# Output projection of a decoder layer: seven half-size products with sums of its weights kept in DRAM

## The chip, the cores and the metric

The kernel runs on one NeuronCore of a Trainium2 chip. A core has five engines with queues of their own: TensorE (PE, matmul), VectorE (DVE), ScalarE (ACT), GpSimd (POOL) and SyncE (SP, which issues nearly all DMAs here), and 16 DMA engines. The metric is the device time of one execution in microseconds; smaller is better. Several runs are taken and their median is compared.

## The reference

One layer of a decoder trunk, 1024 tokens, width 1024, all float32:

```
x = x + 1/2 * SwiGLU_1(RMSNorm(x))
z = RMSNorm(x) @ W_in                        # u, v, c_q, c_kv, k_rope, q_mem, three gates
y_a, y_b, y_c = spatial gating, latent attention, memory attention
merged = sum_i sigmoid(gate_i) * (y_i @ W_branch_i)
x = x + merged @ W_out                       # 1024 x 1024 by 1024 x 1024
x = x + 1/2 * SwiGLU_2(RMSNorm(x))
```

## The kernel before, in words

**Matmul in three parts.** Values are float32, but PE is fed fp32r operands. Each operand is split into `hi` (a cast on ACT) and `lo` (source minus `hi`, on DVE); `split`, L138 to 142. A product is three matmuls, hi hi, hi lo and lo hi, added up in PSUM (`mm3`, L155 to 161). One matmul here has 128 rows of stationary weights and 512 moving columns (tokens).

**Layout.** Activations are feature by token: 8 tiles of 128 features, in two halves of 512 tokens. `Rows` holds the residual stream as `[half, p]`, a tile of 128 x 2 x 512 for two feature tiles.

**Stages in order.** FFN 1 up (`up`, units of two feature columns), FFN 1 down (`down`, 7 loops of 6 steps), the gate and latent projections (`Gates`), mixer branches A and C with attention B among them, branch B with the merge, the output projection (`project`, L1143), FFN 2 up and down. Up, down and gates already are seven half-size products instead of eight (`Seven`, L1398): a 2 x 2 block product is made from seven products of sums of blocks, where the sums of weights (`sums`, names s1 to s4) and of rows (t1 to t4) are made on DVE.

**Branch B and projection before.** `branch_pairs` (L553) makes for each of 8 feature tiles and 2 token halves the product of attention's output with `w_branch` (4 k-steps of 3 matmuls), multiplies it with the gate rows on DVE (L573), adds what branches A and C left (`mc`) on POOL (L574) and splits the result into `merged`. `project` then runs over 2 token halves and 8 output tiles: it loads and splits a column of `w_out` (128 x 1024, again for each half), makes 8 k-steps of 3 matmuls into one PSUM bank, adds the bank to the residual rows (L1155), and calls `norm.feed` (a square on ACT, an addition into the norm's accumulator on DVE, L1302 and L1307). In the second half it runs the norm of the first half as tasks: `sums` (token sums by four PE transposes and a reduce, then an inverse root of ten small DVE operations), `turn` (four PE transposes that spread the scale over partitions, L425), and `part(0)`, `part(1)`: gain and scale on four row pairs (L1344), a difference (L1367) and splits (L147), which give the operands `b22` and `t3` for the first unit of FFN 2.

**The first units of FFN 2** (`units`, L1522) begin with the products of `t3` and `b22`. After `count + 1` = 3 of their k-steps PE takes the token sums of half 1 (`norm.tokens(1)`, L394), so that norm's chain runs beside the rest of these products.

**What sets the order.** Tile's scheduler places instructions by priority (program order) and a model of time; inside `manual_schedule` the engines named keep the written order. In `down` of FFN 1 that is PE, SP, DVE and ACT; in `project` and branch B none. In `down` each step writes: the matmuls of the step, the operand differences (L2101, L2105), the splits for the next step (`prepare`), the row additions due (`acts`), and then what a table `post` holds for that (loop, step); `pre` comes ahead of the matmuls. `pre` at (5, 2) has the norm's token sums (PE transposes at L410). `post` at (1, 0) and (1, 4) fetches gate unit 0 and makes its four sums (L1443). Each step also does a little of the rotary tables.

**Room.** Tags have fixed numbers of buffers: `raw` 3, `whi` and `wlo` 5 each, `t` (rows of 512) 6, `h4` 16, `x4` 10, `w4` 11 (in each FFN's own pool), PSUM `bank` 4 and `one` 4.

**Small jobs.** `rounded` (L691) loads a tile of weights, splits it and stores both parts to DRAM, in two steps at two units; `weight_jobs` (L716) lays them over the units of the first up projection, `Gates.run` others over its units. `spill` (L2061) makes differences of hidden rows on POOL after every second unit.

## Time and profile before

| | |
|---|---|
| median of 3 runs | 2162.38 us (2162.04 to 2163.84) |
| profiled execution | 2163.03 us, of which the span from first to last instruction is 2161.3 |
| granted PE clock | 0.999 |
| up 1, down 1, gates | about 116 to 440, 440 to 651, 651 to 960 us |
| branch B, projection | 1395 to 1440, 1440 to 1527 us |
| DVE busy in 1398 to 1441, to 1484, to 1527 | 38.4, 21.7, 32.7 us of 43 each |

The profile is one execution, seen by the hardware. Its page gives busy time by engine, the chain of work that ended last, and the costliest groups of instructions. Rows of the timeline read: start, time, engine, line, operation, output<-inputs, shape, count, and in brackets how long the engine had been idle and what released it. Busy durations of matmuls overlap, since a matmul starts before the one ahead has left the array; the distance of starts is what one costs.

### The profile page before, as it was taken

The page shows a single profiled execution, that of the slowest core. Times are in us where ns is not written, and L with a number is a line of the kernel's source. Part 1 is how long each engine was busy: PE and PEld are TensorE (multiplying, and loading weights), DVE is VectorE, ACT ScalarE, POOL GpSimd, SP SyncE. Part 2 cuts the span into 40 slices and gives each one's busy share as a digit, 9 for nine tenths or more (in the row PEclk, how much of TensorE's full clock was granted, in tenths as well). Part 3 has the DMA queues.
Part 4 walks back from the last instruction along what each step waited for, and adds up shares of the span by engine and source line. Part 5 has one row for each costly group of instructions (what it writes and reads, how often), then busy time and mean ns, then how long its engine had stood idle before and what let it go on. Part 6 is the DMA issues. An engine that isn't in the chain of part 4 may idle for free.

```text
span 2161.3 us, 27448 instructions
## 1 busy us (share of the span) xinstructions
PE 2151.9 (100%) x10112; PEld 1797.8 (83%) x10112; DVE 1572.1 (73%) x2371; ACT 910.3 (42%) x1486; POOL 255.0 (12%) x256
## 2 busy tenths in 40 slices
PE   9999999999999999999999999999999999999999
PEld 6888888888887888888988889988888888888887
DVE  7966666679889657655786679886876666657884
ACT  6433333243455434433555378833433223224332
POOL 0011111100000000000123311240011212110000
PEclk9999999999999999999999999999999999999999
DMA  4264555385332445641587832293133332347443
GB/s 148 92 220 159 190 180 175 119 318 193 118 124 94 147 164 180 223 149 61 212 283 259 314 105 69 75 348 104 40 127 103 110 97 100 103 144 288 169 129 104
DMA packets 137175, 342.56 MB, mean 158 GB/s; under 512 B 21713, under 2 KB 30033, under 8 KB 137041
## 3 DMA queue, kind: packets, MB, share of 16 engines
q1 hardware_dynamic: 136896, 340.81, 45.9%
q8 instruction: 79, 1.29, 0.2%
q14 instruction: 56, 0.45, 0.1%
q10 hardware_dynamic: 144, 0.00, 0.0%
HBM read 230.90 MB, written 109.86 MB: 158 GB/s over the span
## 4 chain that ended last, share of the span: by engine, by line
PE 91%; DVE 6%; ACT 1%; DMA 1%; issue 1%; SPq 0%; POOL 0%; ACTq 0%; DVEq 0%; POOLq 0%
PE one L158 15%; PE one L159 15%; PE one L160 15%; PE bank L158 13%; PE bank L159 13%; PE bank L160 13%; PE mm L158 1%; PE mm L159 1%; PE mm L160 1%; PE bank L1019 1%; PE one L1967 1%; DVE w L147 1%; DVE wlo L147 1%; DVE pr L997 1%; DVE wlo L142 1%
## 5 line engine op out<-in xcount | busy, mean ns | idle before, releaser
L146 ACT CAST whi<-x 128x1024 fp32r<-128x1024 f32 x202 | 192.3, 955 | 414.4 <-DVE x L1443 170.4
L147 DVE TENSOR_TENSOR wlo<-x,whi 128x1024 fp32r<-128x1024 f32 x202 | 241.2, 1195 | 58.9 <-ACT whi L146 19.6
L1471 DVE TENSOR_TENSOR t<-t,one 128x512 f32<-128x512 f32 x188 | 128.9, 686 | 190.8 <-PE one L160 190.7
L158 PE MATMUL bank<-h,whi 128*128 128x512 f32 x636 | 247.9, 390 | 0.0
L160 PE MATMUL bank<-h,wlo 128*128 128x512 f32 x636 | 247.5, 389 | 0.0
L159 PE MATMUL bank<-h,whi 128*128 128x512 f32 x636 | 247.5, 389 | 0.0
L158 PE MATMUL one<-h,whi 128*128 128x512 f32 x508 | 199.0, 392 | 0.0
L159 PE MATMUL one<-h,whi 128*128 128x512 f32 x508 | 198.4, 390 | 0.0
L160 PE MATMUL one<-h,wlo 128*128 128x512 f32 x508 | 198.3, 390 | 0.0
L158 PE MATMUL one<-w,whi 128*128 128x512 f32 x432 | 168.5, 390 | 0.0
L159 PE MATMUL one<-w,whi 128*128 128x512 f32 x432 | 168.1, 389 | 0.0
L160 PE MATMUL one<-w,wlo 128*128 128x512 f32 x432 | 168.1, 389 | 0.0
L142 DVE TENSOR_TENSOR wlo<-w,whi 128x1024 fp32r<-128x1024 f32 (+2 forms) x112 | 114.4, 1036 | 67.3 <-ACT whi L139 67.1
L139 ACT CAST whi<-w 128x1024 fp32r<-128x1024 f32 (+2 forms) x112 | 98.8, 901 | 149.8 <-PE one L159 55.6
L2067 POOL TENSOR_TENSOR raw<-raw 128x512 f32<-128x512 f32 x38 | 57.0, 1499 | 794.8 <-DVE raw L1908 684.8
L160 PEld LDWEIGHTS bank<-h,wlo 128*128 128x128 f32 x636 | 119.4, 188 | 24.9
L159 PEld LDWEIGHTS bank<-h,whi 128*128 128x128 f32 x636 | 119.4, 188 | 24.6
L158 PEld LDWEIGHTS bank<-h,whi 128*128 128x128 f32 x636 | 119.4, 188 | 24.4
L158 PE MATMUL bank<-whi 128*128 128x512 f32 x352 | 136.9, 389 | 0.0
L159 PE MATMUL bank<-wlo,whi 128*128 128x512 f32 x352 | 136.9, 389 | 0.0
L160 PE MATMUL bank<-whi,wlo 128*128 128x512 f32 x352 | 136.9, 389 | 0.0
L160 PEld LDWEIGHTS one<-h,wlo 128*128 128x128 f32 x508 | 95.8, 189 | 20.1
(406 smaller groups left out, 4892.2 us busy)
## 6 DMA issues: line engine op xcount, KB each, us to landing
x<-in_ffn_w_gu_dram SPq DMA_DIRECT2D x78, 512.0 KB, 5.1
w<-tdt SPq DMA_DIRECT2D x40, 512.0 KB, 4.2
gate<-raw SPq DMA_DIRECT2D x33, 512.0 KB, 3.0
tdb<-raw SPq DMA_DIRECT2D x64, 256.0 KB, 2.1
h<-in_ffn_w_down_dram SPq DMA_DIRECT2D x64, 256.0 KB, 6.0
w<-tdb SPq DMA_DIRECT2D x30, 512.0 KB, 5.1
tdt<-w SPq DMA_DIRECT2D x48, 256.0 KB, 2.4
x<-in_w_gate_dram SPq DMA_DIRECT2D x22, 512.0 KB, 5.9
```

The source lines that it names most:

```text
L139: i = self.nc.scalar.copy(hi, src)
L142: return (eng or self.nc.vector).tensor_tensor(lo, src, hi.bitcast(F32), op=ALU.subtract)
L146: self.nc.scalar.copy(hi, src)
L147: return lambda: self.nc.vector.tensor_tensor(lo, src, hi.bitcast(F32), op=ALU.subtract)
L158: i = mmul(out, s[0], m[0], start=first, stop=False, **kw)
L159: mmul(out, s[0], m[1], start=False, stop=False, **kw)
L160: self.last = mmul(out, s[1], m[0], start=False, stop=last, **kw)
L997: nc.vector.tensor_tensor_reduce(out=pr[:, :m], in0=sc[:, :m], in1=self.mask[:, m0:m0 + m], scale=1.0, scalar=-NEG, op0=ALU.add, op1=ALU.m ...
L1019: nc.tensor.transpose(b[:, at:at + P], prs[t][:, kk * P:(kk + 1) * P], self.ident)
L1471: return self.nc.vector.tensor_tensor(out, x, y, op=ALU.add)
L1967: k.last = nc.tensor.matmul(b, w, norm.x(half, c), start=c == 0, stop=c == DT - 1)
L2067: sub = lambda d, x, y: (eng or nc.gpsimd).tensor_tensor(d, x, y, op=ALU.subtract)
```

## The change

The projection becomes seven products too: `merge` replaces the last call of `branch_pairs` and `project`. With A the blocks of W_out and b those of `merged` (b11 is features 0 to 511 of token half 0, b12 of half 1, b21 and b22 the other features), it makes b11 A11, t2 s2, t1 s1, b22 s4, t3 s3, b21 A12 and t4 A22, each into four banks of 512 tokens with 4 k-steps. A bank that is used by more than one output is added with its sign into several rows. The residual halves change names (norm half 0 is now token half 1), and `store` follows.

The sums s1 to s4 of W_out's blocks are made from DRAM to DRAM, by DMAs on POOL's queue that copy or add (`out_sums`: eight steps of two 512 KB transfers, one step at every odd unit of the first up projection). All seven weight blocks are then split and stored as hi and lo in DRAM by 14 jobs: three in the up projection, eight in `down` (`out_jobs`, split at every second step from (2, 3) to (4, 5)), three in the gates. `merge` only loads them.

Moved: the fetch and the four sums of gate unit 0 go from (1, 0) and (1, 4) to (4, 4) and (5, 1) of `down`; x1d's rows, and the fetch of FFN 2's first weights, from ahead of the projection to places in `merge`; FFN 2's first sums and "t" splits from `units` into `merge` (`later`). The branch additions go from POOL to DVE. PE is in written order in `merge`. The turned sums and the scale of norm half 0 use PSUM tag `one`.

The core of the diff (`weights(n)` in it loads the hi and lo of block n, `add` adds a bank to a row, `put` splits rows into an operand):

```diff
+        sums = self.out_sums()
+        self.wo_parts = self.out_parts()
+        wo = [self.rounded(x.unsqueeze(1), d) for x, d in self.wo_parts[:2] + self.wo_parts[10:11]]
-        for first, some in ((0, jobs), (1, small)):
+        for first, step, some in ((0, 2, jobs), (1, 2, small), (13, 2, wo[:2]), (16, 1, wo[2:])):
...
+        for n, f in enumerate(sums):
+            when[2 * n + 1].append(f)
...
+    def out_sums(self):
+        self.wosum = [self.dram.tile([2, P, D], F32, name=f"wosum{n}") for n in range(4)]
+        A11, A12, A22, A21 = range(4)
+        w, (s3, s1, s2, s4) = self.a["w_out"], self.wosum
+        steps = ((s3, A11, None), (s1, A21, None), (s3, A21, 1), (s1, A22, 1),
+                 (s2, s3, None), (s2, A22, 1), (s4, s2, None), (s4, A12, 1))
+        def step(d, src, more):
+            for g in range(2):
+                x = w[g, src] if isinstance(src, int) else src[g]
+                self.nc.gpsimd.dma_start(d[g], x, max_dma_last_dim=2 * D, **({"accum_op": ALU.add} if more else {}))
...
+    def out_jobs(self, parts):
+        def job(src, dst):
+            x = self.raw()
+            self.nc.sync.dma_start(x, src)
+            yield
+            hi, lo = self.wide("whi"), x.bitcast(F32R)
+            self.split(hi, lo, x)
+            for d, t in zip(dst, (hi, lo)):
+                self.nc.sync.dma_start(d, t.bitcast(F32))
+            yield
+        when = {}
+        for i, part in enumerate(parts):
+            j, q = job(*part), 11 + 2 * i
+            for at, k in ((q, 1), (q + 4, 0)):
+                when.setdefault(at, []).append((k, lambda j=j: next(j)))
...
+    def merge(self, yb, mc, room, norm, load, early, later, sink):
...
+        raw = {n: [room() for _ in range(2)] for n in names}
...
+        def branch(name, k):
...
+            sig, d = self.row(), raw[name][k // 2]
+            nc.sync.dma_start(sig, self.sig[DT + dt][:, hf])
+            if k % 2 == 0:
+                nc.sync.dma_start(d, mc[dt:dt + 2, :, hf].rearrange("k p t -> p k t"))
+            b = self.bank()
+            self.branch(b, w[dt], yb, hf)
+            tt(sig, sig, b, op=ALU.mult)
+            tt(d[:, k % 2], d[:, k % 2], sig, op=ALU.add)
...
+        load()
+        w2 = weights(1)
+        for u, b in product("a", self.single, ws, "b11", True):
+            add(1, 2 * u + 1, b, ALU.subtract)
...
+        for u, b in product("y", self.bank, ws, "t3", True):
+            add(0, 2 * u + 1, b)
+            norm.feed(0, 2 * u + 1)
+            sink(0, 2 * u + 1)
+        ws = weights(6)
+        later()
+        norm.take = self.single
+        for u, b in product("a", None, w2, "b21", False):
+            add(1, 2 * u, b)
+            if u == 1:
+                with self.tc.high_priority(offset=600):
+                    norm.sums(0)
+            elif u == 3:
+                norm.turn(0)
+                norm.take = None
+                norm.part(0)
+            norm.feed(1, 2 * u)
+        for u, b in product("y", None, ws, "t4", False):
+            parts = 2 if u == 3 else 1
+            if u == 0:
+                norm.part(1)
+            add(1, 2 * u + 1, b, parts=parts)
+            norm.feed(1, 2 * u + 1, parts)
+            sink(1, 2 * u + 1)
...
-                    {(1, 0): [do(gates.first, 0)], (1, 4): [do(gates.sums, 0)],
+                    {(4, 4): [do(gates.first, 0)], (5, 1): [do(gates.sums, 0)],
...
-                    late)
+                    late, self.out_jobs([*self.wo_parts[2:10]]))
...
+            def later():
+                for f in range(2):
+                    ffn.sums(f)
+                    made[f] = ffn.weights(f, "t")
+            with tc.manual_schedule(engines={mybir.EngineType.PE}):
+                self.merge(yb, mc, ffn.w4, norm, load, early, later, lambda half, c: keep(x2d, norm.t, half, c))
...
-                    (0, 1), (), ([(0, "a")], [(1, "a")]),
+                    (0, 1), made, ([(0, "a")], [(1, "a")]),
...
+        wo = [k.rounded(x.unsqueeze(1), d) for x, d in k.wo_parts[11:]]
+        jobs = {0: [rows], 1: [rows], 2: [wo[0]], 3: [wo[0], wo[1]], 4: [wo[1], mem[0]], 5: [mem[0], pairs[0]],
+                6: [pairs[0]], 7: [mem[1]], 8: [mem[1], pairs[1]], 9: [pairs[1]], 10: [cq], 11: [cq],
+                12: [wo[2]], 13: [wo[2]]}
```

More of the change, by code (lines that the diff above doesn't have):

```diff
@@ L399, in token_sums, with turned_sums @@
         return b
-    def turned_sums(self, acc, parts=1, late=False):
+    def turned_sums(self, acc, parts=1, late=False, bank=None):
         nc, n = self.nc, acc.shape[-1] // P
@@ L407, in turned_sums @@
             m = min(4, n - t0)
-            b = self.bank()
+            b = (bank or self.bank)()
             for t in range(m):
@@ L1136, in mixer @@
         yb = self.attention(self.branch_pairs(2, yc, md, self.x4, first + each[8:], sink_c))
[L1137 to L1162 removed]
+        return yb, mc
@@ new lines, in out_sums @@
+    def out_sums(self):
[8 more added lines that the diff above has]
+                self.nc.gpsimd.dma_start(d[g], x, max_dma_last_dim=2 * D, **({"accum_op": ALU.add} if more else {}))
+        return [lambda x=x: step(*x) for x in steps]
@@ L1291, in __init__ @@
         self.acc, self.r, self.s, self.op, self.rows = {}, {}, {}, {}, {}
-        self.more = []
+        self.more, self.take = [], None
     def feed(self, half, c, parts=1):
@@ L1320, in tokens @@
         if half == 0 and not self.scaled:
-            self.s[half] = k.turned_sums(self.acc.pop(half), late=True)
+            self.s[half] = k.turned_sums(self.acc.pop(half), late=True, bank=self.take)
         else:
@@ L1333, in turn @@
         k = self.k
-        self.s[half] = k.norm_scale(self.r[half], late=k.last is not None)
+        self.s[half] = k.norm_scale(self.r[half], late=k.last is not None, bank=self.take)
     def norm(self, half, p):
@@ L1712, in run @@
                     self.row_weights(range(5), [w4, x4, x4, x4, x4])
-                self.extra += self.later[:1] + [lambda x=x: got.append(next(x)) for x in jobs.get(n, ())]
+                self.extra += self.later[:1] + [lambda x=x: got.extend(y for y in [next(x)] if y is not None) for x in jobs.get(n, ())]
                 del self.later[:1]
@@ L2085, in up, with down @@
                     self.spill(f // 2)
-    def down(self, rows, load, sink, pre={}, post={}, aside=iter(())):
+    def down(self, rows, load, sink, pre={}, post={}, aside=iter(()), jobs={}):
         k, nc, KT = self.k, self.nc, self.KT
@@ L2184, in loop @@
                     prepare(n + 1, 0)
-                for act in [*acts[n, s], *post.get((n, s), ())]:
+                for act in [*acts[n, s], *post.get((n, s), ()), *jobs.get((n, s), ())]:
                     act()
```

139 lines of the change are left out of this document (103 added, 36 removed).

## The prediction

> **What bounds the kernel now.** I read the page's busy line and chain first, then TensorE's waits, then windows over the stages that the change touches, then the timeline of VectorE (DVE) in them.
>
> ```profile
> PE 2151.9 (100%) x10112; PEld 1797.8 (83%) x10112; DVE 1572.1 (73%) x2371; ACT 910.3 (42%) x1486; POOL 255.0 (12%) x256
> PE 91%; DVE 6%; ACT 1%; DMA 1%; issue 1%; SPq 0%; POOL 0%; ACTq 0%; DVEq 0%; POOLq 0%
> ```
> ```profile
> PE bank L231 <- POOL ident masks.py:199: 1.5, 1, 1.5
> PE one L158 <- DVE raw L1471: 0.7, 2, 0.5
> ```
>
> TensorE (PE) is the whole chain, and its longest wait after the start is 0.5 us. So a matmul less is worth its full spacing, and anything late at PE costs its full lateness. No slack elsewhere pays for either.
>
> ```profile
> 1516.20 0.39 PE L159 MATMUL bank<-h,whi 128*128 128x512 f32 x1
> 1521.64 0.39 PE L159 MATMUL bank<-h,whi 128*128 128x512 f32 x1
> ```
> ```profile
> 1398.00:1441.00 43.00, 43.00 (x191) 35.60 (x191) 38.38 (x47) 15.53 (x28) 24.77 (x17) 1.00 0.95 350
> 1441.00:1484.00 43.00, 43.00 (x192) 35.61 (x191) 21.68 (x34) 14.56 (x26) 1.63 (x1) 1.00 0.62 229
> 1484.00:1527.00 43.00, 43.00 (x195) 35.60 (x194) 32.71 (x52) 15.40 (x22) 0.00 (x0) 1.00 0.17 62
> ```
>
> The two matmuls are one output block apart, 8 k-steps of 3, so 24 matmuls start in 5.44 us: **0.227 us each**. The printed 0.39 is the time through the array, which overlaps. The windows (columns: width, then PE, weight load, DVE, ACT, POOL busy, granted clock, DMA share, GB/s) are branch B (1398 to 1441) and the two halves of the projection. PE is full at full clock in all three; DVE has room in the projection, and DMA is full in branch B.
>
> **What is removed.** The projection is 16 blocks of 24, 384 matmuls. Seven products of 4 blocks of 4 k-steps of 3 are 336. 48 x 0.227 = **10.9 us** off PE; the branch products stay 192. By the busy durations it would be 48 x 0.39 = 18.7 us, which overcounts. The Trainium skill (TensorE: Matmul & The Clock Gate, section Back-to-back issue gap) gives 131 ns for a sustained stream of load and matmul pairs at 512 columns, against 216 ns for a matmul by itself. This stream of pairs shows 227 ns, so here the trace speaks for the second; by the first the saving would be an estimated 6.3 us and the sum below would end 4.6 us later.
>
> **What DVE costs per operation.** Four neighbours without a gap:
>
> ```profile
> 534.93 1.28 DVE L2101 TENSOR_TENSOR h<-h,h 128x512 f32<-128x512 f32 x2
> 536.14 1.29 DVE L142 TENSOR_TENSOR wlo<-h,whi 128x512 fp32r<-128x512 f32 x2
> 537.34 1.22 DVE L142 TENSOR_TENSOR wlo<-w,whi 128x1024 fp32r<-128x1024 f32 x1
> 538.48 0.68 DVE L2218 TENSOR_TENSOR x<-x,w 128x512 f32<-128x512 f32 x1
> ```
>
> Start to start: 0.60 us for 512 columns, 1.14 for 1024.
>
> **The new stage as a whole.** PE needs 192 + 336 matmuls, 119.9 us. DVE: 16 branches of multiply and add, 19.2; four branch weights, 4.8; seven operand splits of two tiles, 16.0; operand sums (8 of 1024), 9.1; 36 block additions, 21.6; 14 norm additions, 8.4; FFN-2 weight sums and two splits, 7.1; norm, about 15. That is 101 us of 120: it fits. The branch additions leave POOL, whose 16 filled most of its 24.8 us there. The Trainium skill (SBUF — State Buffer, section Who interferes with whom) says that a DVE instruction with two SBUF inputs contends with a POOL instruction that reads SBUF. The trace agrees with that:
>
> ```profile
> 1416.94 1.79 POOL L574 TENSOR_TENSOR x<-x,t 128x512 f32<-128x512 f32 x1 [1.97 <-DMA t<-mc]
> 1417.50 1.78 DVE L142 TENSOR_TENSOR h<-x,h 128x512 fp32r<-128x512 f32 x1
> ```
>
> A split of 0.68 us takes 1.78 beside a POOL addition. What DVE gains there it spends on the 16 additions, and I count nothing for it.
>
> **Where it does not fit: the norm of the first output half.** The norm scale of half 0 is turned by PE after the *sixth* product; call its end T. Before, 192 matmuls (43.5 us) followed it; now only the seventh product does, 48 x 0.227 = 10.9 us. After T, DVE must do `part(0)` and `part(1)`:
>
> ```profile
> L1344 DVE SCALAR_TENSOR_TENSOR x<-x,c_ffn_norm,bank 128x512 f32<-128x512 f32 x8 | 5.4, 744 | 0.0
> L147 DVE TENSOR_TENSOR h<-x,h 128x1024 fp32r<-128x1024 f32 x4 | 4.8, 1223 | 0.0
> L1367 DVE TENSOR_TENSOR x<-x,x 128x1024 f32<-128x1024 f32 x2 | 2.4, 1223 | 0.0
> ```
> ```profile
> 1526.40 0.39 PE L159 MATMUL bank<-h,whi 128*128 128x512 f32 x1
> 1527.05 0.75 DVE L1155 TENSOR_TENSOR x<-x,bank 128x256 f32<-128x256 f32 x2 [3.31 <-PE bank L160]
> 1528.02 0.76 DVE L1307 TENSOR_TENSOR t<-t 128x256 f32<-128x256 f32 x2 [0.21 <-ACT t L1302]
> 1528.89 0.95 PE L394 MATMUL bank<-ones,t 128*128 128x1 f32 x8
> ```
>
> The first three rows are exactly these two calls in the old kernel: 12.6 us. Beside them stand the last column of the sixth product and three of the seventh (addition and norm addition, 1.2 each: 4.8) and the last column in halves (0.75 + 0.76 = 1.5). Sum 18.9 us, so the token sums of half 1 are complete at T + 19.0. PE reaches the token sums (L394, now after three k-steps of the first unit, `count=2`) at T + 0.4 (four turns) + 10.9 + 9 x 0.227 = T + 13.3. PE then waits **5.7 us**. The old tail had DVE idle for 3.31 us ahead of the last addition, and PE came just as the sums were done (1528.78 against 1528.89), so nothing absorbs it. The order in which DVE takes these does not matter, since PE needs them all. What was made early (`later`: the unit's sums and "t" splits) is already out of this sum; with it the wait would be 7 us longer. Bounds: 4.7 us if the parts run at the bare spacing (8 x 0.60 + 6 x 1.14 = 11.6); 8 us if `later`'s two "t" splits (2.3) are held up to T by their buffers, which the products' weights use too.
>
> **The down projection.** Gate unit 0's four sums move from step (1, 4) to (5, 1), in DVE's written order ahead of the addition that completes norm half 0, for which PE waits at (5, 2):
>
> ```profile
> 495.91 0.69 DVE L1443 TENSOR_TENSOR x<-raw 128x512 f32<-128x512 f32 x1
> 498.64 0.22 DVE L325 TENSOR_SCALAR t<-t 128x128 f32<-128x128 f32 x1
> ```
> ```profile
> 598.87 1.48 DVE L1307 TENSOR_TENSOR t<-t 128x512 f32<-128x512 f32 x2
> 601.47 0.60 PE L410 MATMUL bank<-ident,t 128*128 128x128 f32 x4
> ```
>
> The four take 2.7 us (first row to second). The last addition ended at 600.35, 1.1 us before PE came. So PE waits 2.7 - 1.1 = **1.6 us**; 0 if DVE is ahead by then, 3 if the last job's split (1.14) is not absorbed.
>
> The eight split jobs there add one cast of 1024 on ACT and 1.14 us on DVE each, at (2, 3) and every second step to (4, 5), with three 512 KB transfers each on SP. DVE is nearly full in that place:
>
> ```profile
> 495.00:552.00 57.00, 57.00 (x253) 47.23 (x252) 55.94 (x104) 21.44 (x33) 0.00 (x0) 1.00 0.48 154
> 530.75 0.39 PE L158 MATMUL one<-whi 128*128 128x512 f32 x1
> 548.13 1.22 DVE L142 TENSOR_TENSOR wlo<-w,whi 128x1024 fp32r<-128x1024 f32 x1 [0.41 <-ACT whi L139]
> 552.00:590.00 38.00, 38.00 (x169) 31.46 (x169) 32.49 (x47) 18.00 (x27) 0.00 (x0) 1.00 0.37 116
> ```
>
> A step is 24 x 0.227 = 5.44 us, and loop 3 starts at 530.75. DVE has its step 2 ready at 538.48 and its step 4 at 548.13 + 1.14 = 549.27; PE wants them at 541.6 and 552.5, so there are 3.2 us to spare. Up to there four jobs add 4.6 us; the four sums no longer ahead of this stretch give 2.7 back, and DVE is idle again from 548. So I take 0 (cover: the 3.2 us); without the cover up to 1.5 us. SP issues a job's stores only after its split, with the fetches three steps ahead (16 us) queued behind; they land in 4 to 7 us. Cost 0.
>
> **The first up projection and the gates.**
>
> ```profile
> 200.00:380.00 180.00, 180.00 (x795) 148.97 (x794) 120.98 (x152) 59.26 (x74) 27.52 (x20) 1.00 0.51 174
> 157.82 1.29 POOL L2067 TENSOR_TENSOR raw<-raw 128x512 f32<-128x512 f32 x1 [16.38 <-DVE raw L1908]
> 700.00:960.00 260.00, 260.00 (x1162) 215.16 (x1161) 167.30 (x236) 107.97 (x132) 12.46 (x6) 1.00 0.52 176
> ```
>
> Six split jobs of 1.14 us meet DVE at 65%. The sixteen DRAM-to-DRAM transfers (8 MB, half of them adding) are issued by POOL, two per odd unit; POOL idles about 16 us ahead of its subtractions, and each sum waits for one issued two units (38 us) earlier; the spill's subtractions stand behind a waiting one. DMA is at half. I take 0. No POOL transfer is in this trace, so the bounds are 0 and the first of the rivals.
>
> **The entry of the merge.**
>
> ```profile
> 1395.30 0.40 PE L158 MATMUL bank<-x,whi 128*128 128x512 f32 x1
> 1402.44 0.82 SPq L1426 DMA_DIRECT2D w<-in_ffn_w_gu_dram  x2
> t<-gate SPq DMA_DIRECT2D x32, 256.0 KB, 5.3
> raw<-in_w_out_dram SPq DMA_DIRECT2D x16, 512.0 KB, 4.0
> ```
>
> The branch accumulators now live in `w4`, whose first write of the old kernel comes 7.1 us after the branch's first matmul, when attention's tiles are free. So the first additions wait till about 1408, while PE goes on: four banks, and a bank is free after the multiplication. The weights' hi and lo come as 2 MB per product, 192 GB/s against the 350 shown, with x1d (4 MB) on top in products 1 and 2. I take 0.4 us for both places, bounds 0 and 3.
>
> **Sum.** -10.9 + 5.7 + 1.6 + 0.4 = **-3.2 us**. The profiled execution took 2163.03 us (span 2161.3 and 1.7 around it), so 2159.8. It stands 0.65 above the median of the runs, 2162.38, so I forecast a median of **2159.2**.
>
> **Rivals.**
> 1. *Full gain:* DVE's queue at T is hidden after all and the sums at (5, 1) meet a DVE that is ahead. 2162.4 - 10.9 = 2151.5; with half the waits 2155. For it: DVE has 19 us to spare in the stage. Against: the scale does not exist before T.
> 2. *All given back:* the 5.7 us grow to 8, the entry and the weights cost 2, the down loops 1.5: -10.9 + 8 + 1.6 + 1.5 + 2 = +2.2, 2164.6; the case begins at 2161.5. For it: DVE at 98% in loops 2 and 3, DMA at 0.95 in branch B.
> 3. *Slower:* branch B runs at the pace of its gate rows. There are six row buffers, and now each is held until the accumulator has come too, so a row's life over six is the pace; PE needs 2.72 us per branch, so it decides from 16.3 us. At 20 us the pace is 3.33 and 16 branches lose 9.8 us: 2159.2 + 9.8 = 2169. For it: the first rows would live from PE's start at 1395.3 to about 1408, 13 us. Against: 5.3 us to landing and 2 us of DVE make 7. (POOL held more than 16 us by a pair of its transfers would have the same sign: 4 us over, in 8 units, is +32.)
> 4. *The change does not do what it says:* if PE still issued 384, +7; the diff leaves no room for it.
>
> **Chances.** Forecast (-1 to -6 us) 0.45; full gain or most of it 0.18; given back 0.22; slower 0.15. A difference of 0.2%, 4.3 us, is about what the measurement tells from none; -3.2 lies inside, and a little under half of the forecast's own spread beyond it. Faster 0.18 + 0.22 = 0.40, same 0.23 + 0.19 = 0.42, slower 0.15 + 0.03 = 0.18. The forecast's own range is 2156 to 2162; to hold 8 in 10 it reaches from 2152.0 to 2166.0.
>
> **What would show it.** 10,064 matmuls and weight loads or so instead of 10,112; a PE wait of 4 to 8 us at the token sums (released by DVE's norm addition), with DVE full for 19 us ahead of it; a wait of 1 to 2 us at the transposes of step (5, 2); none in the first up projection and the gates; POOL without the 16 additions. I am wrong if PE shows no wait at the token sums, or if waits over 2 us stand among the branch or the first products.

## The result, and the profile after

The changed kernel takes **2178.54 us** (median of 6 runs, 2175.93 to 2182.22) against 2162.43 for the kernel before on the same chip (6 runs). The ratio is **1.0075, interval 1.0062 to 1.0088**: 16 us slower, where 2159.2 was forecast. The profiled execution is the fastest of the six, 2175.93 us with a span of 2174.2, 12.9 more than the span before. Of all executions told of below, one (of `before_three_repeats`, 7747 us) is far from the rest and is set aside.

The page's busy line and chain, and PE's waits:

```profile
PE 2147.7 (99%) x10064; PEld 1790.2 (82%) x10064; DVE 1589.1 (73%) x2395; ACT 910.5 (42%) x1466; POOL 241.8 (11%) x256
PE 86%; DVE 8%; DMA 3%; ACT 1%; issue 1%; SPq 0%; POOL 0%; ACTq 0%; DVEq 0%; POOLq 0%
```
```profile
PE bank L410 <- DVE t L1476: 4.7, 1, 4.7
PE bank L158 <- DVE t L1216: 3.5, 1, 3.5
PE bank L231 <- POOL ident masks.py:199: 3.3, 1, 3.3
PE one L159 <- DVE h L147: 3.2, 1, 3.2
PE bank L2138 <- DVE x L2114: 2.2, 1, 2.2
PE bank L1024 <- DVE wlo L142: 1.2, 2, 1.0
```

The 48 matmuls are gone (10112 to 10064), so the change did what it says. But PE, which was the whole chain, now waits 2 us or more in five places, two of them in the first 13 us. PE's own landmarks, in us from the start, tell where the time went. The steps (5, 2) and (5, 3) are those of the down projection; at the turn PE spreads the norm's scale.

| PE reaches | before | after | later by |
|---|---|---|---|
| the first token sums | 14.97 | 19.94 | 5.0 |
| the transposes of (5, 2), start of its wait | 601.47 | 606.99 | 5.5 |
| the turn of (5, 3) | 607.37 | 619.02 | 11.7 |
| the last attention product | 1391.42 | 1404.20 | 12.8 |
| the token sums behind the merge | 1528.89 | 1540.72 | 11.8 |

From the last attention product to the token sums 10.9 us of matmuls are saved, and 1.0 of it arrives.

**The start.** POOL's timeline, and windows of the first 50 us (the columns as in the prediction), the kernel before last:

```profile
1.40 1.41 POOL L1156 DMA_DIRECT2D wosum<-in_w_out_dram  x2 [0.35 <-issue]
2.88 0.34 POOL masks.py:199 TENSOR_SCALAR_AFFINE_SELECT ident<-ident 128x128 f32<-128x128 f32 x1
...
70.34 0.92 POOL L1156 DMA_DIRECT2D wosum<-in_w_out_dram  x1 [7.14 <-issue]
```
```profile
0.00:50.00 50.00, 44.54 (x145) 26.18 (x146) 33.18 (x57) 26.46 (x41) 9.69 (x22) 0.93 0.89 265
```
```profile
0.00:50.00 50.00, 48.04 (x167) 29.77 (x168) 38.09 (x61) 30.27 (x44) 2.37 (x11) 0.97 0.47 159
```

The sum transfers are written at odd units of the up projection, but only PE is in written order there. POOL had nothing else, so the scheduler put all sixteen into the first 71 us. There they share the DMA engines with the first rows of x (share 0.89 instead of 0.47), and two of them stand ahead of the identity matrix that PE begins with.

**Step (5, 2).** VectorE ahead of PE's wait of 4.65 us, and the windows behind it:

```profile
608.24 0.68 DVE L1612 TENSOR_TENSOR x<-raw 128x512 f32<-128x512 f32 x1
608.96 0.69 DVE L1612 TENSOR_TENSOR raw<-raw,x 128x512 f32<-128x512 f32 x1
609.69 0.69 DVE L1612 TENSOR_TENSOR x<-raw 128x512 f32<-128x512 f32 x1
610.29 0.68 DVE L1612 TENSOR_TENSOR raw<-raw 128x512 f32<-128x512 f32 x1
610.90 0.68 DVE L1476 TENSOR_TENSOR t<-t 128x512 f32<-128x512 f32 x1
```
```profile
610.00:612.00 2.00, 0.36 (x2) 0.37 (x3) 1.58 (x3) 0.36 (x1) 0.00 (x0) 0.82 0.95 288
612.00:614.00 2.00, 2.00 (x8) 1.71 (x7) 1.11 (x4) 0.00 (x0) 0.00 (x0) 0.50 0.94 353
614.00:616.00 2.00, 2.00 (x9) 1.58 (x8) 1.79 (x9) 0.00 (x0) 0.00 (x0) 0.83 0.13 51
```

The four sums are 2.66 us (608.24 to 610.90). The other 2 us are lag: without the sums the last addition would have ended at 608.9, 1.9 us after PE came, where that of the kernel before ended 1.1 ahead of PE. At the end of the wait the granted clock falls to 0.5 for 3.4 us; the three shares lost are (0.18 + 0.50 + 0.17) x 2 = 1.7 us. It falls 0.37 us before the wait ends, so 1.5 of the 1.7 comes on top of the wait.

**Branch B.** VectorE at PE's wait, and SP's issues:

```profile
1438.13 1.34 DVE L1216 TENSOR_TENSOR t<-t,bank 128x512 f32<-128x512 f32 x2 [6.80 <-DMA t<-gate]
```
```profile
1405.85 0.34 SPq L1224 DMA_DIRECT2D whi<-wo  x1
...
1407.67 2.83 SPq L1211 DMA_DIRECT2D t<-gate  x5
...
1423.46 3.62 SPq L1595 DMA_DIRECT2D w<-in_ffn_w_gu_dram  x3
1428.19 4.33 SPq L1211 DMA_DIRECT2D t<-gate  x4
```

VectorE idles 6.8 us for a gate row. That row was issued behind 2 MB of product weights and 1.5 MB of FFN 2's, among others, neither needed yet, and DMA is full (388 GB/s and a share of 1.03 from 1407 to 1442).

**The norm behind the merge.** PE's rows:

```profile
1521.28 0.65 PE L425 MATMUL one<-ident,rs_y 128*128 128x128 f32 x4
...
1540.72 1.05 PE L394 MATMUL bank<-ones,t 128*128 128x1 f32 x8 [0.36 <-DVE t L1476]
```

T is 1521.28 and the token sums start at T + 19.4. The prediction had VectorE done at T + 19.0, and PE there, without a wait, at T + 13.3.

### The profile page after: what moved, and what is told of

The parts are those of the page before. It is cut to its first block, busy times and chain, and to the rows that moved or that the text cites. A ratio compares the mean times of both kernels' runs of the same rounds, so it can differ in the third digit from the quotient of the medians.

```text
span 2174.2 us, 27432 instructions
## 1 busy us (share of the span) xinstructions
PE 2147.7 (99%) x10064; PEld 1790.2 (82%) x10064; DVE 1589.1 (73%) x2395; ACT 910.5 (42%) x1466; POOL 241.8 (11%) x256
## 4 chain that ended last, share of the span: by engine, by line
PE 86%; DVE 8%; DMA 3%; ACT 1%; issue 1%; SPq 0%; POOL 0%; ACTq 0%; DVEq 0%; POOLq 0%
PE one L158 15%; PE one L159 15%; PE one L160 15%; PE bank L158 11%; PE bank L159 11%; PE bank L160 11%; DVE wlo L142 2%; PE mm L158 1%; PE mm L159 1%; PE mm L160 1%; DMA invd<-a_inv 1%; DMA t<-gate 1%; PE one L2138 1%; PE bank L2138 1%; PE bank L1024 1%
## 5 line engine op out<-in xcount | busy, mean ns | idle before, releaser
L158 PE MATMUL bank<-h,whi 128*128 128x512 f32 x588 | 229.3, 390 | 0.0
L160 PE MATMUL bank<-h,wlo 128*128 128x512 f32 x588 | 228.9, 389 | 0.0
L159 PE MATMUL bank<-h,whi 128*128 128x512 f32 x588 | 228.8, 389 | 0.0
L159 PE MATMUL one<-h,whi 128*128 128x512 f32 x540 | 211.4, 392 | 3.2 <-DVE h L147 3.2
L158 PE MATMUL one<-h,whi 128*128 128x512 f32 x540 | 212.0, 393 | 0.2 <-ACT h L146 0.2
L160 PE MATMUL one<-h,wlo 128*128 128x512 f32 x540 | 211.3, 391 | 0.0
L160 PEld LDWEIGHTS bank<-h,wlo 128*128 128x128 f32 x588 | 110.4, 188 | 23.0
L159 PEld LDWEIGHTS bank<-h,whi 128*128 128x128 f32 x588 | 110.4, 188 | 22.8
L158 PEld LDWEIGHTS bank<-h,whi 128*128 128x128 f32 x588 | 110.4, 188 | 22.6
L159 PEld LDWEIGHTS one<-h,whi 128*128 128x128 f32 x540 | 101.9, 189 | 25.4 <-DVE h L147 4.1
```

What stands on the lines that cost most here:

```text
L158: i = mmul(out, s[0], m[0], start=first, stop=False, **kw)
L159: mmul(out, s[0], m[1], start=False, stop=False, **kw)
L160: self.last = mmul(out, s[1], m[0], start=False, stop=last, **kw)
```

## The experiments

Medians below stand against the kernel before on the same chip (2162.5 to 2163.2 in these calls) and the changed kernel's 2178.5; the changed kernel was not run again beside them. All edits are to the changed kernel, if nothing else is said.

### The transfers: three other places, and alone

```diff
# sums_in_order (also: written at units 6, 8, ... 20)
-                self.nc.gpsimd.dma_start(d[g], x, ...)
+                i = self.nc.gpsimd.dma_start(d[g], x, ...)
+                self.after(i, self.last)
# sums_in_gap: behind the last subtraction of a spill
+                self.after(i, behind)
# sums_in_idle_dma: behind the landing of unit 2's weights
+            k.loaded = nc.gpsimd.tensor_copy(k.stat("loaded", 1), self.quad[2][1][:, 0, :1])
+                self.after(i, self.loaded)
# before_with_transfers: the kernel before, the sixteen transfers added, their results unused
+        self.out_sums()
```

> The changed kernel with one edit: the sixteen DRAM-to-DRAM transfers of the weights' sums are put behind matmuls of the first up projection's units 6, 8, ... 20, so that POOL issues the first of them behind its first subtractions, about 120 us in, instead of within the first 71 us. If the 5.0 us that the changed kernel is behind at its first token sums come from these transfers (they fill the DMA queues while the first rows of x are loaded, and hold POOL before the identity mask), the first token sums come back from 19.9 to about 15 us, PE's wait for x falls from 2.2 to under 0.5 us and that for the identity from 3.3 to 1.5, and the whole is about 5 us faster than the changed kernel. Rival: only the late identity mask counts; then it is the same here, since the mask is early again too, but the wait for x stays at 2 us. Second rival, the one the prediction gave: POOL is held by its transfers in the up projection; then waits of PE on the spilled operands or of DVE on raw buffers show there, 4 us per pair, and the whole is slower.

> The changed kernel with one edit: each of the eight pairs of sum transfers is issued by POOL right behind the fourth subtraction of a spill (units 5, 7, ... 19), where POOL then idles 12 to 16 us. In the run before it (transfers behind matmuls of the even units) the second transfer of a pair was issued some 9 us after the first, with POOL standing still in between, and where a subtraction stood behind it PE waited (1.4, 0.5 and 0.7 us). Theory: POOL is held about 9 us by each pair, so in the gap it costs nothing: the first token sums at about 15 us, no PE wait over 0.2 us between 80 and 600 us, and the whole 4 to 5 us faster than the changed kernel. Rival: the transfers also slow SP's loads in the up projection (DMA at 0.6 to 0.7 there), and PE's waits of 0.5 to 1.4 us stay whatever POOL does.

> The changed kernel with one edit: POOL's sum transfers wait for the last of the first loads (a one-column copy on POOL reads the weights of unit 2, which land at about 27 us), so that they fall between 27 and 100 us, where the kernel before shows DMA shares of 0.00 to 0.17. Theory: the transfers cost PE time only through the DMA queues that they share, at the start with the rows of x (5 us), in the up projection with the stores of the split jobs, whose buffers the next weights wait for (4.3 us of waits in the run with the transfers in POOL's gaps). In a stretch where DMA is idle they cost nothing: the first token sums at about 15 us, no PE wait over 0.7 us between 80 and 600 us (the waits from 1.9 us up, each with its 1.7 us of clock, stay as they are at (5, 2), in branch B and at the token sums), and PE reaches the transposes of (5, 2) 5 us earlier than in the changed kernel. The whole is 4 to 6 us faster, plus or minus a clock loss of 1.7. Rival: accumulating transfers cost PE in some other way wherever they run; then 2 to 4 us of waits show up in 27 to 100 us or behind it.

> The kernel before, with the sixteen DRAM-to-DRAM transfers of the weights' sums added (on the weights as the kernel before has them; nothing reads the results) and nothing else changed; POOL issues them from the start. If they alone make the changed kernel's loss at the start, the first token sums come at about 20 instead of 15 us, and the whole is 5 to 6.5 us slower than the kernel before, with PE waiting 2 to 3 us for x. Rival: the loss in the changed kernel comes from elsewhere in its start; then the whole is within 2 us of the kernel before.

Measured: 2174.84 (ratio 1.0052, 1.0037 to 1.0067), 2180.43 (1.0086, 1.0071 to 1.0101), **2172.17** (1.0042, 1.0029 to 1.0056), and 2169.99 for the kernel before with the transfers (1.0035, 1.0022 to 1.0048: 7.0 us slower).

Alone, the transfers cost 7.0 us, a little more than the 5 to 6.5 expected. Put in order, the start is mended (first token sums 4.9 us earlier), but PE waits 1.4, 0.5 and 0.7 us in the up projection. In POOL's gaps these waits add up to 4.3 us, so the theory of the held POOL fell. The rows of that run, POOL's first, then what VectorE waited for in 200 to 400 us and the stores' landing there; the last fence has the same store in the kernel before:

```profile
216.00 0.93 POOL L1155 DMA_DIRECT2D wosum<-in_w_out_dram  x1
226.91 0.92 POOL L1155 DMA_DIRECT2D wosum<-in_w_out_dram  x1 [9.97 <-issue]
```
```profile
DVE wlo L147 <- DMA wkv<-wlo: 25.8, 5, 6.5
```
```profile
wkv<-wlo SPq DMA_DIRECT2D x5, 512.0 KB, 7.6
```
```profile
wkv<-wlo SPq DMA_DIRECT2D x5, 512.0 KB, 4.9
```

POOL does stand still for 10 us between two transfers, but what reaches PE is the rival: a split job's store lands in 7.6 us instead of 4.9, keeps its `wlo` buffer, and the next unit's weights wait for that buffer (VectorE 25.8 us in all, 11.1 in the kernel before). In a stretch where DMA idles (share 0.09 from 30 to 90 us before) the same sixteen cost nothing that shows: 6.4 us come back, behind the identity's 1.5 us no wait up to (5, 2) is over 0.7, and PE comes to (5, 2) at 601.27 us (601.47 in the kernel before).

### The down projection

```diff
# gate_sums_later
-{(4, 4): [do(gates.first, 0)], (5, 1): [do(gates.sums, 0)],
+{(4, 4): [do(gates.first, 0)], (5, 2): [do(gates.sums, 0)],
# job_lows_on_pool
-            self.split(hi, lo, x)
+            self.split(hi, lo, x, self.nc.gpsimd)
# sums_later_jobs_earlier: the first edit, and
-            j, q = job(*part), 11 + 2 * i
+            j, q = job(*part), 8 + 2 * i
# before_sums_at_5_1: the kernel before
-(1, 4): [do(gates.sums, 0)],
+(5, 1): [do(gates.sums, 0)],
```

> The changed kernel with one edit: gate unit 0's four sums stand at step (5, 2) of the down loops, behind the norm scale's arithmetic, instead of at (5, 1) ahead of the last norm addition. Theory: DVE's four sums (2.66 us) are part of PE's wait of 4.65 us at the transposes of (5, 2), and the rest is lag that DVE has gathered from the last split jobs. Then the wait falls to about 2.0 us, the granted clock after it drops less, and the whole is 2.7 to 4 us faster than the changed kernel. Rival A: the sums account for all; the wait is under 0.5 us and the whole 5 to 6 us faster. Rival B: the sums only move on and delay the scale's turn at (5, 3); the wait there grows from 0.7 us by about 2, and the whole is the same.

> The changed kernel with one edit: the subtraction of each of the down loops' eight split jobs (128 x 1024, 1.14 us of DVE) runs on POOL, which is idle there. Theory: PE's wait of 4.65 us at (5, 2) is the four sums (2.66, of which 1.1 meet slack) and about 3 us that DVE has gathered from the last three jobs; without them the wait is 1.6 us, as the prediction had it, and the whole about 3 to 4 us faster. Rival A: DVE's lag comes from the casts on ScalarE and the stores on SP that a job adds, and these stay; then the wait stays at 4 us or more. Rival B: POOL's reads slow DVE's operations with two SBUF inputs beside them, as a split beside a POOL addition took 1.78 us for 0.68 in branch B; then DVE loses as much as it gains, and the wait stays as well.

> The changed kernel with two edits in the down loops: gate unit 0's sums at (5, 2) as before, and the split jobs begin three steps earlier, at (1, 2), so that the last three subtractions fall ahead of the stretch in which DVE idles (about 566 to 582 us). Theory: the 2.2 us of wait that were left at (5, 2) with the sums alone moved are the lag of the last jobs; then this wait is under 0.5 us, the clock loss behind it (1.7 or 3.4 us in every run with a wait there of 2.2 us or more) is gone, and the whole is 7 to 9 us faster than the changed kernel. Rival: DVE, full in loops 2 and 3, passes the lag to PE there instead; then PE waits 2 us or so on a wlo split between 530 and 565 us, and the whole is no faster than with the sums alone moved (about 2174).

> The kernel before with one part of the change alone: gate unit 0's four sums move from step (1, 4) of the down loops to (5, 1), ahead of the last norm addition. No split jobs, no other change. The prediction's step, 2.7 us of sums against 1.1 us of slack: PE waits 1.6 us at the transposes of (5, 2). If the clock falls only behind waits of about 2 us or more, the loss ends there: 1.6 us, 2164 or so. Rival: DVE is not ahead by 1.1 us any more, or falls behind further, and the wait is 3 us or over, with 1.7 to 3.4 us of clock loss behind it, 2167 to 2169.

Measured: 2173.92 (1.0050, 1.0035 to 1.0065), 2183.73 (1.0096, 1.0083 to 1.0110), **2173.22** (1.0056, 1.0040 to 1.0071) and, in the kernel before, 2163.96 (1.0006, 0.9998 to 1.0015). The wait at (5, 2) in PE's waits of the first, the third and the last:

```profile
PE bank L410 <- DVE t L1476: 2.2, 1, 2.2
```
```profile
PE one L159 <- DVE wlo L142: 0.5, 1, 0.5
PE bank L410 <- DVE t L1476: 0.5, 1, 0.5
```
```profile
PE bank L410 <- DVE t L1307: 1.2, 1, 1.2
```

Alone, the move of the four sums costs a wait of 1.2 us and no clock: the prediction's step (1.6) was right by itself. Without the sums 2.2 are left, and with the jobs three steps earlier 0.5: the rest came with the jobs. But that run is only 0.7 us below the first, and 5.3 below the changed kernel where 7 to 9 were expected. With the jobs earlier, some of PE's matmuls between 526 and 590 us start 0.3 to 0.9 us apart instead of 0.23, 2.4 us more in all: part of the rival, a lag that VectorE passes to PE earlier. The jobs' subtractions on POOL are worse. POOL's and VectorE's rows of that run:

```profile
579.32 2.41 POOL L142 TENSOR_TENSOR raw<-raw,whi 128x1024 fp32r<-128x1024 f32 x1 [12.99 <-ACT whi L139]
```
```profile
579.74 3.14 DVE L142 TENSOR_TENSOR wlo<-h,whi 128x512 fp32r<-128x512 f32 x2 [2.16 <-ACT whi L139]
```

Two splits that take 1.28 us take 3.14 beside POOL, PE waits 2.0 us in the loops and 5.3 at (5, 2). The Trainium skill (SBUF — State Buffer, section Who interferes with whom) has VectorE's second port shared with GpSimd under an exclusive lock; this pair of rows agrees.

### Branch B

```diff
# merge_loads_behind
-                    nc.sync.dma_start(t.bitcast(F32), src)
+                    self.after(nc.sync.dma_start(t.bitcast(F32), src), self.last)
...
+                self.after(...)     # the same for x1d's rows and FFN 2's first weights
```

> The changed kernel with one edit: in the merge the loads of the product weights, of the rows of x1 and of FFN-2's first two units are put behind the matmuls beside which they are written, so that SP issues the gate rows and branch values ahead of them. Theory: branch B's wait of 3.5 us (and the 2 to 3 us of thin matmuls around it) comes from the DMA queues, full at about 385 GB/s from 1407 to 1442 us because 8 MB or so that is not needed yet goes ahead of the gate rows. Then the wait for the branch multiplication is under 0.5 us, no gate row is waited for by DVE for over 1 us after the first, and the whole is 4 to 6 us faster than the changed kernel. Rival (the prediction's third): a row's life, held until the branch accumulator has come, sets the pace whatever the order; then PE's wait stays over 2 us. Second rival: the wait moves to the products, which then wait for weights or x1 rows.

Measured: **2172.82** (1.0038, 1.0024 to 1.0052), 5.7 us less than the changed kernel. PE has no wait over 0.2 us in branch B. Gate rows land in 5.2 us and the branch values in 8.3, where the changed kernel has 6.9 and 10.6:

```profile
t<-gate SPq DMA_DIRECT2D x16, 256.0 KB, 5.2
w<-mc SPq DMA_DIRECT2D x8, 512.0 KB, 8.3
```

The prediction's third rival is a part of this. In the changed kernel the first six gate rows live 15.8 to 19.5 us, from issue to the addition into the accumulator, mostly over the 16.3 us that it named, because the branch values come late; with the loads behind, they live 10.9 to 16.9. So a row's life took part, and the order of the loads set it: the rival as put here, "whatever the order", falls. The seventh row, which PE waits for, was also issued some 4 us after the first buffer was free, behind FFN 2's weights.

### The norm behind the merge

```diff
# turn_earlier
-            if u == 1:    # norm.sums(0)
+            if u == 0:
-            elif u == 3:  # norm.turn(0)
+            elif u == 2:
# first_products_by_half: k-steps of pair 0 first, and
-turn=5, ... count=2)
+turn=11, ... count=7, by=lambda x: x[2] // 2)
```

> The changed kernel with one edit: in the sixth product the token sums of output half 0 stand behind the first output block instead of the second, and the turn of its scale behind the third instead of the fourth, so that VectorE can begin the two norm parts 2.7 us earlier in PE's order. Theory: VectorE's queue behind the turn is what PE waits for (3.2 us at t3's low part and 0.4 at the token sums of half 1), so these fall by about 2.5 us together, with perhaps 0.6 us of new wait at the token sums of half 0; the whole is 2 to 3 us faster. Rival: VectorE is full through the sixth product already (products' additions and splits), so the norm parts start no earlier, the wait stays at 3 us or moves to the token sums of half 0, and the whole is the same within 1 us.

> The changed kernel with one edit: FFN-2's first two units take the k-steps of the first row pair (t3 and b22, part 0) of all four products ahead of those of the second pair, and the token sums of output half 1 stand behind the eighth instead of the third k-step, the turn behind the twelfth. Theory: PE waits 3.2 us for t3's second pair because VectorE makes it last, and for the token sums 0.4; with eight k-steps (5.4 us) instead of two (1.4) ahead of the second pair PE arrives 4 us later, so both waits are under 0.5 us. The scale of half 1 is then turned 4 us later, and a part of that comes back as a wait at the products of b11. The whole is 1.5 to 3 us faster. Rival: all comes back behind the turn (the chain root, turn, norm of b11 and its split is as long as the rest of the products), and the whole is the same within 1 us.

Measured: 2180.11 (1.0081, 1.0065 to 1.0097) and 2181.32 (1.0087, 1.0074 to 1.0100). Neither gains. In the first the turn stands 2.7 us earlier in PE's order, 0.8 of which goes to a new wait at the token sums of half 0. But one column of the sixth product now stands behind it in VectorE's queue: from the turn to the token sums of half 1 it is 21 us instead of 19.4, and the wait of 3.2 became 0.8, 0.4, 2.5 and 1.2. In the second the wait of 3.15 stayed, since PE meets it at the second matmul of the unit, which is for pair 0, and 0.9, 0.6 and 1.3 us came behind the turn.

### Do waits cost more than their length?

```diff
# before_three_repeats: the kernel before
+(5, 1): [do(gates.sums, 0)] * 3,
```

> The kernel before, with gate unit 0's four sums made as before at (1, 4) and then three times over again at (5, 1) (the same values, twelve VectorE operations of about 0.6 us, put there only to make PE wait). 3 x 2.4 to 2.66 less 1.1 us of slack: PE waits 6.1 to 6.9 us at the transposes of (5, 2). If a long wait costs its length alone, the whole is 6.5 us slower than the kernel before. If the granted clock falls behind it, it is 8.2 to 9.9 us slower (1.7 or 3.4 more), with a lower clock in the 4 to 8 us behind the wait and nowhere else.

Measured: 2171.62 (1.0039, 1.0026 to 1.0052), 8.6 us slower, with one wait of 6.55 us. Its windows:

```profile
606.00:608.00 2.00, 0.00 (x0) 0.00 (x0) 1.93 (x4) 0.00 (x0) 0.00 (x0) 0.50 0.05 18
608.00:610.00 2.00, 1.11 (x5) 1.11 (x6) 0.84 (x2) 0.00 (x0) 0.00 (x0) 0.50 0.00 0
610.00:612.00 2.00, 2.00 (x7) 1.52 (x6) 1.71 (x8) 0.00 (x0) 0.00 (x0) 0.50 0.00 0
612.00:614.00 2.00, 2.00 (x10) 1.60 (x9) 1.93 (x6) 0.00 (x0) 0.00 (x0) 0.91 0.00 0
```

Half the clock from 606 to 612, part of it while PE still waits: against the kernel before, PE is 7.4 us late at the transposes and 9.1 at the turn one step later. So this wait cost its length and 1.7 us.

### The repairs together

```diff
# all_four: sums_in_gap, gate_sums_later, job_lows_on_pool, merge_loads_behind and first_products_by_half
# three_repairs: sums_in_idle_dma, sums_later_jobs_earlier and merge_loads_behind
# three_repairs_pool_adds: the same, and in the norm of half 1, columns 0 to 6
-                    k.nc.vector.tensor_tensor(acc[half][:, n], acc[half][:, n], sq[:, n], op=ALU.add)
+                    k.nc.gpsimd.tensor_tensor(acc[half][:, n], acc[half][:, n], sq[:, n], op=ALU.add)
# t_weights_elsewhere: three_repairs, and
-                    made[f] = ffn.weights(f, "t")
+                    made[f] = ffn.weights(f, "t", self.x4)
```

> The changed kernel with the edits together: sum transfers in POOL's gaps, gate unit 0's sums at (5, 2), job subtractions on POOL, the merge's loads behind, FFN-2's first products by half. If the parts add up as told apart, about 5 (start) + 6 (down) + 5 (branch B) + 2 (token sums) = 18 us come back of the changed kernel's 2178.5, so about 2160, 2 to 3 us below the kernel before. If the seven products' 10.9 us are all there, nothing else of the change costs, and the waits are all undone, it is 2151.5. Rival: the waits are fed by one another (PE that is earlier at one place is too early at the next), and it stays above the kernel before, at 2165 or more.

> The changed kernel with the repairs that belong to the causes found: transfers behind the first loads, gate unit 0's sums at (5, 2) with jobs three steps earlier, the merge's loads behind. If the parts add up (5 at the start, 4.65 and 1.7 to 3.4 of clock in the down loops, 3.5 and 1.7 of clock and 1 of thin matmuls in branch B), 17 us of 16 to 18 come back and it is 2160 to 2162; with the seven products' 10.9 us less the 5.4 that PE loses to VectorE at the token sums it should then lie 2 to 5 us below the kernel before, 2157 to 2160. Rival: the loss is passed on to later waits, as in the run of all four edits, and it stays above 2168.

> The kernel with the three repairs and one more edit: seven of the eight norm additions of output half 1 (0.60 us of VectorE each) run on POOL, which idles in the products. Theory: from the turn of half 0's scale to the token sums of half 1 VectorE's queue of 19 us is what PE waits for; with 4 or 5 of its additions gone that is 2.4 to 3 us shorter, and the waits at t3's low part and the token sums together (3.5) fall to about 1, with no clock loss behind them (1.7): 2.5 to 4 us faster than the three repairs alone. Rival: POOL's reads slow VectorE's operations with two SBUF inputs (0.68 to 1.78 us for a split, in branch B of the kernel before), so VectorE gains nothing and the waits stay within 0.5 us of what they were.

> The kernel with the three repairs and one more edit: the early t splits of FFN-2's first two units are written to x4 tiles instead of the buffers that the product weights use. In VectorE's order no weight split then stands between the turn of half 0's scale and the token sums of half 1 (one of 1.14 us did, for unit 0's a part), and the t split of unit 1 comes behind the root of half 1. Theory: VectorE's 19 us there is what PE waits for, so the wait (3.1 us) falls by about 1.1 us to 2.0, at the edge of where the clock loss begins: 1.1 us faster than the three repairs with the clock loss, up to 2.8 or 4.5 without. Rival: the split that now stands behind the root delays the norm of half 1, and the wait moves there: no change.

Measured: 2180.05 (1.0080, 1.0067 to 1.0092); **2164.22** (1.0006, 0.9998 to 1.0015; 11 runs); 2164.93 (1.0007, 0.9998 to 1.0016); 2165.56 (1.0017, 1.0008 to 1.0026). The first joined three edits that lose by themselves to two that gain. The three repairs gave 6.4, 5.3 and 5.7 us singly, 17.4 in sum, and together 14.3: level with the kernel before, where 2157 to 2160 was expected. In their run PE has no wait over 0.3 us from 1395 us to the last matmul of the seventh product. The branch's first matmul and that last one, then the last matmul of the projection in the kernel before, whose branch begins at 1395.30:

```profile
1399.01 0.40 PE L158 MATMUL bank<-x,whi 128*128 128x512 f32 x1
1519.63 0.39 PE L160 MATMUL bank<-h,wlo 128*128 128x512 f32 x1
```
```profile
1526.62 0.39 PE L160 MATMUL bank<-h,wlo 128*128 128x512 f32 x1
```

From first to last it is 120.6 us instead of 131.3: the seven products save 10.7 us. What is left in this run besides: PE begins the branch 3.7 us late, 2.3 of it from starts further apart ahead of (5, 2), as above, 0.5 from the wait there; the rest was not traced. Then comes the norm. PE's longest waits and the windows there:

```profile
PE one L159 <- DVE h L147: 3.1, 1, 3.1
PE bank L231 <- POOL ident masks.py:199: 1.5, 1, 1.5
```
```profile
1520.00:1525.00 5.00, 1.64 (x5) 1.10 (x5) 5.00 (x8) 3.75 (x7) 0.00 (x0) 0.75 0.78 321
1525.00:1530.00 5.00, 5.00 (x16) 3.51 (x15) 3.24 (x7) 0.00 (x0) 0.00 (x0) 0.50 0.00 0
1530.00:1535.00 5.00, 5.00 (x19) 3.97 (x19) 3.60 (x11) 0.00 (x0) 0.00 (x0) 0.73 0.01 3
```

In this execution the token sums are 1.0 us ahead of the kernel before; then the clock is at half for 10 us, and at the next turn (1533.20 against 1531.88) it is behind. The two last edits tried to shorten VectorE's queue. POOL's additions slowed VectorE's operations beside them (three splits took 4.57 us in a row, 3.5 without them), and the wait stayed (2.9 and 0.4). The splits moved elsewhere turned it into 2.0, 1.9, 0.4, 0.9 and 0.9. No version has a median below that of the kernel before.

## Why the prediction was wrong

**The term that failed most is the 0 for "The sixteen DRAM-to-DRAM transfers (8 MB, half of them adding) are issued by POOL, two per odd unit".** They were not: POOL's place in the order was the scheduler's, and it was the start of the kernel, at 5 us there (7.0 in the kernel before with them alone). The second half of the step, "DMA is at half. I take 0", failed too: where the transfers did run beside the units, a store's landing went from 4.9 to 7.6 us and PE waited 4.3 us in all. The rival's price for a held POOL (32 us) was far too high; the mechanism that counted was not in the prediction.

**"So PE waits 2.7 - 1.1 = 1.6 us" at (5, 2)** was near alone (1.2) and wrong with the jobs: 4.65, and 1.5 of clock. The failing step is "Up to there four jobs add 4.6 us ... So I take 0": it asked whether loops 2 and 3 could take four jobs, and did not carry their lag to the wait that it ends at. The bound of 3 us named one job's split; it was short by that and the clock.

**The entry of the merge, 0.4 with a bound of 3,** measured 3.5, and 5.7 came back when the loads were put in order. The prediction counted the bytes over whole products, where they fit; it did not ask in which order SP, free in `merge`, would send them. Its third rival had the mechanism, a row held until its accumulator comes, and was set aside with "5.3 us to landing and 2 us of DVE make 7"; the first rows lived 15.8 us and more. A wait over 2 us among the branch products was one of its signs of being wrong.

**The wait at the token sums, 5.7,** was right in its mechanism: VectorE's queue held the token sums until T + 19.4, and so PE came 6.1 us later than T + 13.3. Its waits (3.2 and 0.4, with 0.2 for ScalarE) and 1.5 of clock are 5.2 of that; the rest is in no row. VectorE's last addition ends at T + 19.7 for T + 19.0, with two misses of opposite sign: one of `later`'s two splits (1.14 us), which the sum had left out and only the bound of 8 held, stood in the queue, and the norm's parts took 12.1 us for 12.6. The wait fell mostly one row earlier than said, at t3's low part.

**The -10.9** is there: with three terms mended, branch and products take 10.7 us less than branch and projection did, and the kernel before is reached in spite of the loss at the norm.

**No term stood for the clock.** The prediction priced a wait of PE at its length. Behind that for the identity, four waits of 2 us or more stand in the profiled run, three of them with a half clock of 3.4 us, which is up to 1.7 us lost; the runs' spread (2175.93 to 2182.22) and granted clocks (0.997 to 0.993, against 0.999) fit more of these in the slower ones, and that is the likely difference between the profiled pair (12.9) and the medians (16.1). That part is argued, not shown.

Open: PE's wait at L1024 in attention (0.2 us before, 1.0 after, up to 1.9 and 3.8 in single runs, 0.2 in several) was not traced to a cause, nor was the extra 1 us behind the last matmul.

## What to carry to other kernels

Before costing a moved DMA, ask which engine's order is written and which is the scheduler's: a transfer that nothing holds back goes to the earliest place its queue allows, ahead of loads that are needed first. Follow a chain of added work to the next wait that ends late, not to the next place with slack, and count a wait of PE of 2 us or more as some 1.7 us longer than it is, at times more (a loss behind 40 of 43 here, as told below).

## What the hardware showed that was not expected

The granted clock falls to a half for 3.4 us (1.7 us lost where PE works) or a multiple of that. In the eighteen profiles of this study, the wait for the identity at the start left aside, 40 of 43 PE waits of 1.95 us or more have such a loss within a few microseconds, and none of the nine that stand alone at 1.2 to 1.9 us has one.

Within one execution these stretches begin on a fixed raster of 3.41 us. In the changed kernel's they begin at 13.94, 44.66, 611.27 and 1536.28 us, the last three 9, 175 and 446 steps behind the first. What sorts the waits is how much of one step PE is idle. At full clock and behind the start, every step with more than 2.0 us of idle PE was followed by a half clock, and of those with 1.0 to 1.7 us none was; between 1.7 and 2.0 both occur. That tells the three exceptions: the 3.47 us of branch B lie 1.80 in one step and 1.67 in the next, the 2.82 of `all_four` lie 1.44 and 1.38, and of the 2.21 of `job_lows_on_pool` 1.97 lie in one. A few falls have another cause that was not found: eight profiles, the kernel before's among them, have one at 38.8 to 44.7 us with PE busy in the step ahead, and why some stretches go on for two or three steps was not worked out.

The Trainium skill (TensorE: Matmul & The Clock Gate, section What's actually happening) gives a half rate decided in free-running windows of 3.4 us. Size, ratio and raster agree; that gaps well under a window suffice is what these runs add.

POOL's DRAM transfers landed in 5.7 us (median) in the stretch where DMA had idled, and in the up projection (200 to 400 us) in 9.5 where they read `w_out`. There POOL issued the second of two copying transfers 0.5 to 0.8 us after the first, and the second of two adding ones 8.0 to 11.9 us after (`sums_in_gap`, 512 KB each).
